# Row scales of the first linear attention moved from q and k to v, and a spread ratio in the gate pair, in a two-layer encoder kernel

## The chip, the cores and the metric

The kernel runs on one core of a Trainium2 chip. The metric is the device time of one execution in microseconds (us), taken as the median of several runs. The core has five engines with queues of their own, each working through its instructions in order: TensorE (PE, with its weight loads shown as PEld), VectorE (DVE), ScalarE (ACT), GpSimd (POOL) and SyncE (SP, which here only issues DMAs). They wait for each other through semaphores. What stands in each queue, and in which order, is fixed when the program is built.

## What is computed

Two layers of an encoder over 256 tokens of width 1024, in float32. What matters here is the first layer's beginning:

```python
u = rms_norm(h, g_mix_pre)
(gq, gk, gv, gg, ra_f, ra_b, aq, ak, av, gate_a, gate_b) = jnp.split(u @ w_in, offsets, axis=-1)
qh = gq * (GLA_DK ** -0.5); kh = gk; vh = gv           # 4 heads of 128, values of 256
# two directions of: scores = mask(q_dec @ k_intra^T); o = scores @ v + inter-chunk part
o_gla = rms_norm(o_f + o_b, g_gla_out)                 # per head
branch_a = (o_gla * silu(gg)) @ w_o_gla
branch_b = gqa_attention(q, k, v) @ w_o_attn           # 8 heads, 2 key/value heads, rope
mixed = sigmoid(gate_a) * branch_a + sigmoid(gate_b) * branch_b
h = h + rms_norm(mixed @ w_out, g_mix_post)            # then a SwiGLU FFN and an embedding step
```

## The kernel before, in words

**Tokens and halves.** The 256 tokens are two halves (`hf` 0 and 1) of 128, a token on each partition. `uT` holds the input of a layer transposed (features on partitions), split into a high part of type fp32r and the rest, so that a float32 product is three matmuls: high by high, high by low, low by high.

**Weights.** They stream through one class, `Stream`. A unit is 512 rows by 512 columns (1 MB): SP loads it into one of two `raw` buffers (L296), ACT casts it to fp32r (`wh`, L132) and DVE subtracts (`wl`, L132), both in two pieces of 128x1024. A `raw` buffer is free for the next load when DVE's second subtraction is done; `wh` and `wl` have four buffers each. Counted from 0, the layer's units 0 to 3 are the decay ranks and the attention's queries (`rq`), 4 and 5 the attention's keys and values (`kv`), 6 and 7 the linear attention's q, 8 and 9 its k (together `gqk`), 10 to 13 its v, 14 to 17 its output gate (`gg`), and then follow the units of gate A, the pair for gate B and `w_o_gla` in turn, in the order of the string `GATES` (21 is the last of gate A). On PE a `gqk` unit is 48 matmuls of 128x256, the others 24 of 128x512.

**The first layer's row scale.** In layer 0, `uT` is made from x before its RMS norm is known, and the factor r = 1/sqrt(mean(x^2)+eps) of each token (`rs[hf]`, made on POOL in `rstd`, L776 to L780, with `he` = 128 eps / r^2) is applied to what comes out of the products. Where tokens lie on partitions it is a scalar of the eviction. The linear attention's q and k come out with features on partitions and tokens along the row (`project_t`), so there the factor must be a row that is the same on every partition. `spread_rows` (L874) makes it: POOL writes a matrix of ones, DVE multiplies the identity by `rs[0]` and by `rs[1]` (L882), PE multiplies ones by these diagonals (two float32 products, four matmuls in the trace, L104 `aux_0kv`), ACT copies the result (L884). It is called right behind the `kv` products (L1090), so its matmuls stand in PE's queue between `kv` and `gqk`, and its two DVE instructions stand in DVE's queue behind what the scheduler put ahead of them. The four results of `gqk` are then evicted by DVE with a multiplication by that row (L1185); layer 1 evicts them on ACT (L1190, L1192).

**Around it.** Tasks (generators that yield a number of ticks) put the transposes, scores, softmax and output products of the attention (`attend`, `softmax`) and of the linear attention (`gla`: `decays`, `scores`, `outputs`) between the weight products. The keys are scaled by their norm on DVE (L1075), and the transposed decay ranks are copied to `raT` on DVE (L994). `outputs` (L1269) takes the sum of squares of each head, adds eps and raises to -1/2 on POOL (`inv_sqrt`).

**The gate pair.** Gate B is computed as a two-by-two block product with seven products (`seven`, L627) instead of eight. Its four blocks of the input are the two token halves by the two halves of the features; `whole` (L1380) adds high and low again, `sums` (L602) makes the four mixed forms and splits them, and two of the seven products (the sixth and the seventh) take their blocks straight from `uT`.

Of the kernel before, what the change touches and what calls it, by code (L numbers as in the profile page):

```python
# [27 lines left out]

WAIT_NEXT, WAIT_IN, WAIT_H = (7, 11), ((6, 9), (6, 6)), ((3, 5), (3, 5))
WAIT_MIX = 4, 6  # L30
W = dict(r=5, z=6, s0=4, s=3, s1=9, o0=1, o=1, k=4, q=3, a0=1, a1=4, a2=4, a3=1, g=6)

STEPS_FIRST = "00 10 01 11 02 12 03 13".split()
# [25 lines left out]
def trunk_kernel(ctx: ExitStack, tc: tile.TileContext, a: dict, out: bass.AP):  # L59
# [564 lines left out]

        return made, Task(make(), part[0])

    def seven(sp, forms, gated):  # L627

        made, task = forms
        quad = lambda hf, j: lambda k: sp.tok(4 * j + k, hf)  # L630
        form = lambda i: lambda k: [p[:, k, :] for p in made[i]]

        def add(out, x, y):
            nc.vector.tensor_tensor(out=out, in0=x, in1=y, op=ALU.add)

        (p1, v), (p3, p7) = (halves(mid()) for _ in range(2))
        c11, p5, o = acc(), acc(), []
        c12, c22 = p3, p7

        def product(i, then):  # L640

            o[:] = [acc()]
            times(o[0], form(i), True, then)

        def both():
            add(v, o[0], v)
            add(c12, v, p3)
            add(c22, v, p7)

        def last():  # L650
            vsub(v, p5, c22)
            gated(1, v, c22)

        times(c11, quad(0, 0), True, lambda: nc.scalar.copy(p1, c11))
        yield
        task.need()
        product(0, lambda: nc.scalar.copy(p3, o[0]))
        yield
        times(p5, form(1), True, lambda: vsub(v, p5, p1))
        yield  # L660
        product(2, lambda: nc.scalar.copy(p7, o[0]))
        yield
        product(3, both)
        yield
        times(c11, quad(0, 1), False, lambda: gated(0, c11, c12))
        yield
        times(p5, quad(1, 1), False, last)
        yield

    def project_t(sp):  # L670
# [87 lines left out]
    warm_up(WARM[1], True)  # L758
    uT = Split()
    ss = [small(2, "ss") for _ in range(2)]  # L760
    rs, he = ([small(1, tag, 2) for _ in range(2)] for tag in ("rs", "he"))
    ropes_first = []

    up_first = [mid()]
# [10 lines left out]
    def rstd(hf):  # L775
        on("pool", nc.gpsimd.tensor_scalar,  # L776
           out=rs[hf], in0=ss[hf][:, 0:1], scalar1=ss[hf][:, 1:2], scalar2=EPS, op0=ALU.add, op1=ALU.add)
        on("pool", nc.gpsimd.tensor_scalar, out=he[hf], in0=rs[hf], scalar1=P * EPS, scalar2=None, op0=ALU.mult)
        on("pool", nc.gpsimd.tensor_tensor, out=rs[hf], in0=rs[hf], in1=neghalf[:, 0:1], op=ALU.pow)
        last_pow[0] = line["pool"]  # L780

    def gains():
# [36 lines left out]
    def start():  # L819
        cut = lambda piece, c: [t[:, c] for t in piece]  # L820
        gains()
        for hf in range(2):
            turn(hf, 0)
        for hf in range(2):
            high(hf, 0)
        warm_up(WARM[2], True)
        turn(0, 1)
        turn(1, 1)
        turn(0, 2, 3)
        for c in RQ:  # L830
            on("act", nc.scalar.copy, *(t[:, slice(*c)] for t in unit_a[::2]))
        rest(0, 0)
        rest(1, 0)
        low(*cut(unit_a, slice(0, 288)))
        high(0, 1)
        high(1, 1)
        low(*cut(unit_a, slice(288, 1056)))
        on("act", nc.scalar.copy, unit_b[0], unit_b[2])
        rest(0, 1)
        rest(1, 1)  # L840
        high(0, 2, 3)
        low(*unit_b)
        rest(0, 2, 3)
        ws.load()
        unit_c, unit_d = ws.pieces()
        yield 2
        turn(1, 2, 3)
        high(1, 2, 3)
        rest(1, 2, 3)
        yield 4  # L850
        split_here(*unit_c)
        split_here(*unit_d)
        ws.load()
        for hf in range(2):
            square(hf, 0)
        yield 2
        turn(0, 4, 5, 6, 7)
        for hf in range(2):
            square_here(hf, 1)
            rstd(hf)  # L860
        ropes_first.extend(rope_tables(0))
        high(0, 4, 5, 6, 7)
        rest(0, 4, 5, 6, 7)
        yield 1
        turn(1, 4, 5, 6, 7)
        high(1, 4, 5, 6, 7)
        rest(1, 4, 5, 6, 7)
        for piece in ws.pieces():
            split_here(*piece)
        ws.load()  # L870
        ws.open = True
        ws.fill()

    def spread_rows():  # L874

        both = mid()
        diag, ones, out = both[:, 0:T], both[:, T : T + P], both[:, 512 : 512 + T]
        nc.gpsimd.memset(ones, 1.0)
        ps = aux()
        for hf in range(2):  # L880
            s = slice(hf * P, (hf + 1) * P)
            nc.vector.tensor_scalar(out=diag[:, s], in0=ident, scalar1=rs[hf], scalar2=None, op0=ALU.mult)  # L882
            mm(ps[:, s], ones, diag[:, s], True, True)
        nc.scalar.copy(out, ps[:, 0:T])  # L884
        return out

    def keep_embedding():

# [43 lines left out]
    for l in range(DEPTH):  # L932

        part[0] = f"{l}rq"
        rows, eps = ([None, None], [None, None]) if l else (rs, he)
        after_start = tc.issue_after(line["dma"].ins) if l == 0 else nullcontext()
        if l == 0:
            ropes = ropes_first
# [28 lines left out]
        def put_ranks(o, hf):  # L967
# [23 lines left out]
            ps = aux()  # L991
            for d in range(2):
                nc.tensor.transpose(ps[0:81, d * P : (d + 1) * P], r[:, d, 0:81], ident)
            nc.vector.tensor_copy(  # L994
                raT[:, :, hf * P : (hf + 1) * P], ps[0:81, 0 : 2 * P].rearrange("p (d t) -> p d t", d=2)
            )

# [6 lines left out]
        def put_q(hf, b, o):  # L1004
            qr, ss = qrs[hf], qss[hf]
            with tc.high_priority(EMPTY if l else EMPTY_FIRST):
                if b == 0:
                    ranks.append(Task(put_ranks(o, hf), part[0]))
                c0, c1 = RQ[b]
                lo = 32 if b == 0 else 0  # L1010
                n, hd = (c1 - c0 - lo) // P, max(c0 - 32, 0) // P
                src, dst = o[:, lo : c1 - c0], qr[:, hd * P : (hd + n) * P]

                with ws.behind(4 + hf, 0) if l == 0 else nullcontext():
                    head_ss(src, n, dst, ss[:, hd : hd + n])
                inv_sqrt(ss[:, hd : hd + n], n, 1.0, P * EPS, eps[hf])
                with ws.behind(4 + hf, 1) if l == 0 else nullcontext():
                    rope(src, n, ropes[0], hf, dst)

        def rq_step(o, hf, b, u):  # L1020
# [41 lines left out]
        def keys(o):  # L1062
            krs = []
            for hf in range(2):
                with tc.high_priority(EMPTY):
                    kr = t512()
                    ss = small(2, "kss")
                    head_ss(o[hf], 2, kr, ss)
                    inv_sqrt(ss, 2, 1.0 / P, EPS, eps[hf])
                    rope(o[hf], 2, ropes[1], hf, kr)  # L1070
                    s = slice(hf * 256, (hf + 1) * 256)
                    split_by(avh[:, s], avl[:, s], o[hf][:, 256:512], rows[hf])
                    for i in range(2):
                        s = slice(i * P, (i + 1) * P)
                        nc.vector.tensor_scalar(  # L1075
                            out=kr[:, s], in0=kr[:, s], scalar1=ss[:, i : i + 1], scalar2=None, op0=ALU.mult
                        )
# [9 lines left out]

        keys = Task(keys(project(uT)), f"{l}kv")
        if l == 0:
            spread = spread_rows()  # L1090


        aT = Split()
# [85 lines left out]
        for x in range(2):  # L1179
            o = project_t(uT)  # L1180
            for i in range(2):
                dst = qk[:, x, 2 * i : 2 * i + 2, :]
                src = o[i].rearrange("p (h t) -> p h t", t=T)
                if l == 0:
                    nc.vector.scalar_tensor_tensor(  # L1185
                        out=dst, in0=src, scalar=1.0 if x else P**-0.5,
                        in1=spread.unsqueeze(1).broadcast_to([P, 2, T]), op0=ALU.mult, op1=ALU.mult,
                    )
                elif x == 0:
                    nc.scalar.activation(dst, src, AF.Copy, bias=0.0, scale=P**-0.5)  # L1190
                else:
                    nc.scalar.copy(dst, src)  # L1192
# [76 lines left out]
        def outputs(hf, pr):  # L1269
# [3 lines left out]
            for i in range(2):  # L1273
# [7 lines left out]
                nc.scalar.activation(  # L1281
                    on[:, hf, c], oh, AF.Square, scale=1.0 / 16.0, accum_out=ss[:, i : i + 1]
                )
            inv_sqrt(ss[:, 0:2], 2, 1.0, EPS)
            for i in range(2):
                hd = 2 * pr + i
                scale_gain(
# [32 lines left out]
        )  # L1320
        for j in range(2):
            for hf, o in enumerate(project(uT)):
                split_by(*(t[:, hf, j * 512 : (j + 1) * 512] for t in v), o, rows[hf])
        valued[0] = True


# [32 lines left out]
        def sigmoid(br, hf, j, src):  # L1359
            if sgate[br] is None:  # L1360
                sgate[br] = big().rearrange("p (s c) -> p s c", s=2)
            with tc.issue_after(last_exp[0].ins):
                by = {} if rows[hf] is None else {"scale": rows[hf]}
                nc.scalar.activation(sgate[br][:, hf, j * 512 : (j + 1) * 512], src, AF.Sigmoid, **by)

        def blocks(sp, then):

            for j in range(2):
                o = [acc(), acc()]
                for kh in range(2):  # L1370
# [6 lines left out]
                    ws.done()  # L1377
                    yield

        def whole():  # L1380

            res = [halves(mid()) for _ in range(2)]
            for hf in range(2):
                for j in range(2):
                    hi, lo = (t.bitcast(F32) for t in uT.at(4 * j, 4, hf * P, P))
                    nc.vector.tensor_tensor(
                        out=res[hf][j].rearrange("p (k t) -> p k t", t=P), in0=hi, in1=lo, op=ALU.add
                    )
            return res

        def gate_b(hf, c0, c1):
# [3 lines left out]
        def merge(br):  # L1395
# [15 lines left out]
        steps = {  # L1411
            "u": blocks(uT, lambda j, hf, o: sigmoid(0, hf, j, o)),
            "m": blocks(gT, merge(0)),
            "s": seven(uT, forms, gate_b),
        }
        for x in GATES:
            if x == "m":
# [236 lines left out]
```

## Time and profile before

| | |
|---|---|
| time, median of 3 runs | 934.36 us (932.77 to 934.6) |
| the profiled execution | 932.52 us, of which its span is 930.7 us |
| busy share of the span | PE 98%, PEld 84%, DVE 85%, ACT 62%, POOL 9% |
| mean granted TensorE clock | 0.992 |
| bytes moved | 173.44 MB, 186 GB/s over the span |

Every engine name in a row is followed by the line of the kernel. `wl_0kv` is a tile named `wl` made in the part `0kv`: the digit is the layer, the rest the stage whose code asked for it, which for weights is often the stage before the one that uses them. `out<-in` names what is written and read. A row of the timeline has the start, the time from the start to the end of a group of equal instructions, the engine, the line, the operation, the tiles, the shapes and the count, and in brackets how long the engine had been idle and what ended that.

### The profile page before, as it was taken

To read this page: it belongs to the slowest core of one execution; us is meant where nothing else is said; L and a number is where in the kernel's file an instruction comes from. 1 tells how busy PE (TensorE), PEld (TensorE's weight loads), DVE (VectorE), ACT (ScalarE), POOL (GpSimd) and SP (SyncE) were. 2 spreads that over 40 slices of the span, in tenths; PEclk is the share of its full clock that TensorE was granted. 3 is DMA by queue.
4 is the path that set the end of the run, shared out by engine and by line. 5 is a ranking of instruction groups with operands and counts; after the bars stand their busy time and mean duration, and the time that the engine had idled before them with its cause. 6 is when DMAs were issued, how large, how long until landed. Compare 5 with 4: busy or idle time off the path is not lost.

```text
span 930.7 us, 12440 instructions
## 1 busy us (share of the span) xinstructions
PE 911.6 (98%) x4676; PEld 777.3 (84%) x4676; DVE 787.6 (85%) x1012; ACT 578.8 (62%) x959; POOL 83.8 (9%) x145
## 2 busy tenths in 40 slices
PE   9879999999999999999999999999999999999996
PEld 8779888888888888888899988888888888888886
DVE  7868989996678998999788789899876799989984
ACT  6647777664476656575676586765644766656563
POOL 2700101130010000000013101110000100000000
PEclk9989999999999999999999999999999999999999
DMA  8552356547468474727666533555573855556361
GB/s 291 182 198 91 97 177 227 165 148 261 136 212 286 136 271 158 271 77 242 246 215 203 179 132 107 165 181 180 182 227 110 280 193 189 217 176 238 126 237 45
DMA packets 88679, 173.44 MB, mean 186 GB/s; under 512 B 3422, under 2 KB 26470, under 8 KB 88108
## 3 DMA queue, kind: packets, MB, share of 16 engines
q1 hardware_dynamic: 88460, 172.40, 55.0%
q8 instruction: 36, 0.59, 0.3%
q10 hardware_dynamic: 160, 0.27, 0.1%
q14 instruction: 23, 0.19, 0.1%
HBM read 169.50 MB, written 3.15 MB: 186 GB/s over the span
## 4 chain that ended last, share of the span: by engine, by line
PE 87%; DVE 4%; DMA 3%; ACT 2%; issue 2%; POOL 1%; SPq 0%; POOLq 0%; DVEq 0%; ACTq 0%
PE acc_0ffnin L120 12%; PE acc_1ffnin L120 11%; PE acc_1gate L120 7%; PE acc_0gate L120 7%; PE acc_0ffnin L104 6%; PE acc_1ffnin L104 6%; PE acc_0gqk L120 3%; PE acc_0wout L120 2%; PE acc_1gqk L120 2%; PE acc_1ple L120 2%; PE acc_1gg L120 2%; PE acc_0gg L120 2%; PE acc_0v L120 2%; PE acc_0merge L120 2%; PE acc_1merge L120 2%; PE acc_1rq L120 2%
## 5 line engine op out<-in xcount | busy, mean ns | idle before, releaser
L104 PE MATMUL acc_0ffnin<-wh_0ffnin,big_0ffnin 128*128 128x512 f32 x176 | 56.9, 393 | 0.0
L104 PE MATMUL acc_1ffnin<-wh_1ffnin,big_1ffnin 128*128 128x512 f32 x176 | 56.8, 392 | 0.0
L132 ACT CAST wh_1ffnin<-raw_1ffnin 128x1024 fp32r<-128x1024 f32 x38 | 38.5, 1049 | 26.0 <-PE acc_1ffnin L104 10.4
L132 ACT CAST wh_0ffnin<-raw_0ffnin 128x1024 fp32r<-128x1024 f32 x38 | 38.4, 1049 | 23.9 <-PE acc_0ffnin L104 9.3
L132 DVE TENSOR_TENSOR wl_1ffnin<-raw_1ffnin,wh_1ffnin 128x1024 fp32r<-128x1024 f32 x38 | 45.0, 1220 | 8.3 <-ACT wh_1ffnin L132 8.2
L132 DVE TENSOR_TENSOR wl_0ffnin<-raw_0ffnin,wh_0ffnin 128x1024 fp32r<-128x1024 f32 x38 | 44.7, 1219 | 7.3 <-ACT wh_0ffnin L132 7.2
L120 PE MATMUL acc_1ffnin<-wh_1ffnin,big_1wout 128*128 128x512 f32 x168 | 42.5, 393 | 0.0
L120 PE MATMUL acc_0ffnin<-wh_0ffnin,big_0wout 128*128 128x512 f32 x168 | 42.5, 393 | 0.0
L104 PEld LDWEIGHTS acc_0ffnin<-wh_0ffnin,big_0ffnin 128*128 128x128 f32 x176 | 33.0, 188 | 7.1 <-DVE big_0ffnin L132 0.5
L104 PEld LDWEIGHTS acc_1ffnin<-wh_1ffnin,big_1ffnin 128*128 128x128 f32 x176 | 33.0, 188 | 6.7
L132 DVE TENSOR_TENSOR wl_0ffnin<-lent_0ffnin,wh_0ffnin 128x1024 fp32r<-128x1024 f32 x30 | 35.8, 1216 | 1.8 <-ACT wh_0ffnin L132 1.8
L132 DVE TENSOR_TENSOR wl_1ffnin<-lent_1ffnin,wh_1ffnin 128x1024 fp32r<-128x1024 f32 x30 | 35.8, 1217 | 1.8 <-ACT wh_1ffnin L132 1.6
L120 PEld LDWEIGHTS acc_0ffnin<-wh_0ffnin,big_0wout 128*128 128x128 f32 x168 | 31.1, 188 | 6.2
L120 PEld LDWEIGHTS acc_1ffnin<-wh_1ffnin,big_1wout 128*128 128x128 f32 x168 | 31.1, 188 | 6.2
L132 ACT CAST wh_1ffnin<-lent_1ffnin 128x1024 fp32r<-128x1024 f32 x30 | 30.7, 1053 | 7.3 <-PE acc_1ffnin L104 3.9
L132 ACT CAST wh_0ffnin<-lent_0ffnin 128x1024 fp32r<-128x1024 f32 x30 | 30.7, 1054 | 7.1 <-PE acc_0ffnin L104 3.9
L104 PE MATMUL acc_0ffnin<-wl_0ffnin,big_0ffnin 128*128 128x512 f32 x88 | 34.2, 389 | 0.0
L104 PE MATMUL acc_1ffnin<-wl_1ffnin,big_1ffnin 128*128 128x512 f32 x88 | 34.2, 389 | 0.0
L132 DVE TENSOR_TENSOR wl_1gate<-raw_1gate,wh_1gate 128x1024 fp32r<-128x1024 f32 x20 | 23.5, 1218 | 6.7 <-ACT wh_1gate L132 6.7
L132 ACT CAST wh_1gate<-raw_1gate 128x1024 fp32r<-128x1024 f32 x20 | 20.0, 1047 | 12.9 <-DMA raw_1gate<-in_w_o_attn_dram 6.1
L132 DVE TENSOR_TENSOR wl_0gate<-raw_0gate,wh_0gate 128x1024 fp32r<-128x1024 f32 x20 | 23.6, 1223 | 4.9 <-ACT wh_0gate L132 4.8
L132 ACT CAST wh_0gate<-raw_0gate 128x1024 fp32r<-128x1024 f32 x20 | 20.0, 1050 | 11.3 <-DMA raw_0gate<-in_w_o_attn_dram 5.4
(702 smaller groups left out, 2693.4 us busy)
## 6 DMA issues: line engine op xcount, KB each, us to landing
raw_0ffnin<-in_w_ffn_out_dram SPq DMA_DIRECT2D x11, 1024.0 KB, 5.4
raw_1ffnin<-in_w_ffn_out_dram SPq DMA_DIRECT2D x11, 1024.0 KB, 5.3
lent_0ffnin<-in_w_ffn_in_dram SPq DMA_DIRECT2D x6, 1024.0 KB, 7.7
lent_1ffnin<-in_w_ffn_in_dram SPq DMA_DIRECT2D x6, 1024.0 KB, 6.5
raw_0v<-in_w_in_dram SPq DMA_DIRECT2D x4, 1024.0 KB, 5.3
raw_0gate<-in_w_o_gla_dram SPq DMA_DIRECT2D x4, 1024.0 KB, 5.1
raw_0gate<-in_w_o_attn_dram SPq DMA_DIRECT2D x4, 1024.0 KB, 5.2
raw_0wout<-in_w_ffn_in_dram SPq DMA_DIRECT2D x8, 512.0 KB, 5.3
```

The source lines that it names most:

```text
L104: return nc.tensor.matmul(o, lhsT, rhs, start=start, stop=stop)
L120: nc.tensor.matmul(o, x, y, start=start and n == 0, stop=stop and n == len(seq) - 1, **kw)
L132: return nc.scalar.copy(hi, src), nc.vector.tensor_tensor(out=lo, in0=src, in1=hi.bitcast(F32), op=ALU.subtract)
```

## The change

For layer 0 only:

- **q and k of the linear attention are no longer scaled by r.** They are evicted on ACT as in layer 1. The factor of k goes to v, whose eviction takes r^2 (`rows2`); the factor of q is dropped, because the outputs are normalised per token and head, with eps replaced by eps/r^2 (`em`).
- **`spread_rows` goes.** `scales` makes `em`, `r2` = r^2 and `rho` = r(half 1)/r(half 0) times a constant on POOL, five instructions of 128x1 behind `rstd`. A task `spread` transposes `rho`, broadcast over 128 columns, with one PE instruction 12 ticks later, and ACT copies it, with the constant taken out, to `even` (a row of 128 ratios, the same on every partition) in the buffer of layer 0's first rope table.
- **In the gate pair** the second token half is multiplied by `even` (two DVE products of 128x512 in `whole`), so that both halves take `rows[0]` in the sigmoid. The seventh product then needs that scaled block too: `alone`, one more buffer of type `mid` and one more split (ACT cast and DVE subtraction of 128x512).
- **From DVE to ACT**: the four evictions, the scaling of the keys by their norm (four of 128x128) and the two copies to `raT`.
- **Order**: the third block of the attention's queries of half 1 has its rope held behind the split of unit 6 instead of unit 5 (`ws.behind`).

```diff
-    def seven(sp, forms, gated):
+    def seven(sp, forms, gated, alone=()):
...
-        times(p5, quad(1, 1), False, last)
+        times(p5, (lambda k: [x[:, k * P : (k + 1) * P] for x in alone]) if alone else quad(1, 1), False, last)
...
+    def scales():
+        for hf in range(2):
+            on("pool", nc.gpsimd.tensor_scalar, out=em[hf], in0=he[hf], scalar1=1.0 / P, scalar2=None, op0=ALU.mult)
+            on("pool", nc.gpsimd.tensor_tensor, out=r2[hf], in0=rs[hf], in1=rs[hf], op=ALU.mult)
+        on("pool", nc.gpsimd.tensor_scalar,
+           out=rho, in0=he[0], scalar1=rs[0], scalar2=rs[1], op0=ALU.mult, op1=ALU.mult)
         last_pow[0] = line["pool"]
...
-    def spread_rows():
-        both = mid()
-        diag, ones, out = both[:, 0:T], both[:, T : T + P], both[:, 512 : 512 + T]
-        nc.gpsimd.memset(ones, 1.0)
+    def spread():
+        yield WAIT_SPREAD
         ps = aux()
-        for hf in range(2):
-            s = slice(hf * P, (hf + 1) * P)
-            nc.vector.tensor_scalar(out=diag[:, s], in0=ident, scalar1=rs[hf], scalar2=None, op0=ALU.mult)
-            mm(ps[:, s], ones, diag[:, s], True, True)
-        nc.scalar.copy(out, ps[:, 0:T])
-        return out
+        nc.tensor.transpose(ps[:, 0:P], rho.broadcast_to([P, P]), ident)
+        nc.scalar.activation(even, ps[:, 0:P], AF.Copy, bias=0.0, scale=1.0 / (P * EPS))
...
-            nc.vector.tensor_copy(
+            (nc.vector.tensor_copy if l else nc.scalar.copy)(
                 raT[:, :, hf * P : (hf + 1) * P], ps[0:81, 0 : 2 * P].rearrange("p (d t) -> p d t", d=2)
...
-                with ws.behind(4 + hf, 1) if l == 0 else nullcontext():
+                with ws.behind(4 + hf + (hf == 1 and b == 2), 1) if l == 0 else nullcontext():
                     rope(src, n, ropes[0], hf, dst)
...
+                        if l == 0:
+                            nc.scalar.activation(kr[:, s], kr[:, s], AF.Copy, bias=0.0, scale=ss[:, i : i + 1])
+                            continue
...
         if l == 0:
-            spread = spread_rows()
+            even = small(512, "rope0", 1)[:, 0:P]
+            Task(spread(), f"{l}kv")
...
-                if l == 0:
-                    nc.vector.scalar_tensor_tensor(
-                        out=dst, in0=src, scalar=1.0 if x else P**-0.5,
-                        in1=spread.unsqueeze(1).broadcast_to([P, 2, T]), op0=ALU.mult, op1=ALU.mult,
-                    )
-                elif x == 0:
+                if x == 0:
                     nc.scalar.activation(dst, src, AF.Copy, bias=0.0, scale=P**-0.5)
...
-            inv_sqrt(ss[:, 0:2], 2, 1.0, EPS)
+            inv_sqrt(ss[:, 0:2], 2, 1.0, EPS, eps_out[hf])
...
-                split_by(*(t[:, hf, j * 512 : (j + 1) * 512] for t in v), o, rows[hf])
+                split_by(*(t[:, hf, j * 512 : (j + 1) * 512] for t in v), o, rows2[hf])
...
-                by = {} if rows[hf] is None else {"scale": rows[hf]}
+                by = {} if l else {"scale": rows[0 if br else hf]}
...
+            if l == 0:
+                for j in range(2):
+                    t = res[1][j].rearrange("p (k t) -> p k t", t=P)
+                    vmul(t, t, even.unsqueeze(1).broadcast_to([P, 4, P]))
+                alone.extend(halves(mid(F32R)))
+                split(*alone, res[1][1])
```

More of the change, by code (lines that the diff above doesn't have):

```diff
@@ L30 @@
 WAIT_MIX = 4, 6
+WAIT_SPREAD = 12
 W = dict(r=5, z=6, s0=4, s=3, s1=9, o0=1, o=1, k=4, q=3, a0=1, a1=4, a2=4, a3=1, g=6)
@@ L760, in trunk_kernel @@
     ss = [small(2, "ss") for _ in range(2)]
-    rs, he = ([small(1, tag, 2) for _ in range(2)] for tag in ("rs", "he"))
+    rs, he, em, r2 = ([small(1, tag, 2) for _ in range(2)] for tag in ("rs", "he", "em", "r2"))
+    rho = small(1, "rho", 1)
     ropes_first = []
@@ L779, in rstd @@
         on("pool", nc.gpsimd.tensor_tensor, out=rs[hf], in0=rs[hf], in1=neghalf[:, 0:1], op=ALU.pow)
+        last_pow[0] = line["pool"]
+    def scales():
[4 more added lines that the diff above has]
+           out=rho, in0=he[0], scalar1=rs[0], scalar2=rs[1], op0=ALU.mult, op1=ALU.mult)
         last_pow[0] = line["pool"]
@@ L860, in start @@
             rstd(hf)
+        scales()
         ropes_first.extend(rope_tables(0))
@@ L934, in trunk_kernel @@
         part[0] = f"{l}rq"
-        rows, eps = ([None, None], [None, None]) if l else (rs, he)
+        rows, eps, eps_out, rows2 = ([[None, None]] * 4) if l else (rs, he, em, r2)
         after_start = tc.issue_after(line["dma"].ins) if l == 0 else nullcontext()
@@ L1378, in blocks @@
                     yield
+        alone = []
         def whole():
@@ L1413, in trunk_kernel @@
             "m": blocks(gT, merge(0)),
-            "s": seven(uT, forms, gate_b),
+            "s": seven(uT, forms, gate_b, alone),
         }
```

## The prediction

> **What bounds the kernel now.** I read the share of each engine in slices of the span first, from the profile's page.
>
> ```profile
> PE   9879999999999999999999999999999999999996
> PEclk9989999999999999999999999999999999999999
> ```
>
> TensorE is at nine tenths or more in nearly all of the 40 slices of 23.3 us. The second and third slices, 23 to 70 us, are among the few that aren't, and in the third its clock dips too. So a change pays only if it shortens PE's queue or takes away time in which PE stands still. The second view is PE's waits from 45 us to 930 us (engine, line, what it waited for, total us, times, longest).
>
> ```profile
> PE aux_0kv L104 <- DVE mid_0kv L882: 9.7, 1, 9.7
> PE aux_1at L104 <- DVE mid_1at L132: 0.2, 1, 0.2
> ```
>
> These are all of them: behind the start, PE waits once for 9.7 us, for the diagonals of `spread_rows`, and never again for more than 0.2. The third view is the timeline around that wait.
>
> ```profile
> 41.77 1.07 PE L120 MATMUL acc_0kv<-wl_0rq,big_start 128*128 128x512 f32 x4
> 41.89 1.21 DVE L132 TENSOR_TENSOR wl_0rq<-raw_start,wh_0rq 128x1024 fp32r<-128x1024 f32 x1
> 43.69 0.41 DVE L994 CAST raT<-aux_0rq 81x256 fp32r<-81x256 f32 x1
> 46.49 0.86 DVE L1075 TENSOR_SCALAR t_0kv<-t_0kv,kss_0kv 128x128 f32<-128x128 f32 x4
> 47.27 2.35 DVE L132 TENSOR_TENSOR wl_0rq<-raw_0rq,wh_0rq 128x1024 fp32r<-128x1024 f32 x2
> 49.88 2.35 DVE L132 TENSOR_TENSOR wl_0kv<-raw_0rq,wh_0kv 128x1024 fp32r<-128x1024 f32 x2
> 52.15 0.47 DVE L882 TENSOR_SCALAR mid_0kv<-ident,rs_start 128x128 f32<-128x128 f32 x2
> 52.57 1.20 PE L104 MATMUL aux_0kv<-mid_0kv 128*128 128x128 f32 x4 [9.73 <-DVE mid_0kv L882]
> 55.92 2.36 DVE L132 TENSOR_TENSOR wl_0kv<-raw_0rq,wh_0kv 128x1024 fp32r<-128x1024 f32 x2 [3.30 <-ACT wh_0kv L132]
> ```
>
> PE ends `kv` at 41.77 + 1.07 = 42.84. The next in its queue are the four matmuls on the diagonals. DVE makes those at 52.15, because by its order they stand behind the splits of units 7 and 8. Yet unit 6, which PE could multiply at 42.84, is split at 41.89 + 1.21 = 43.10. The wait comes from an order, not from missing data. The fourth view is of windows (length, then busy us and count of PE, PEld, DVE, ACT, POOL, then PEclk, DMA share, GB/s).
>
> ```profile
> 45.00:50.00 5.00, 0.00 (x0) 0.00 (x0) 5.00 (x13) 1.98 (x3) 0.47 (x1) 0.54 0.52 192
> 55.00:60.00 5.00, 5.00 (x42) 5.00 (x41) 2.36 (x2) 2.40 (x3) 0.00 (x0) 0.93 0.49 150
> 42.84:82.81 39.97, 30.24 (x242) 30.23 (x243) 29.97 (x58) 20.24 (x42) 1.78 (x3) 0.87 0.49 160
> 82.81:152.27 69.46, 69.46 (x384) 59.60 (x383) 63.22 (x109) 53.85 (x112) 10.35 (x16) 1.00 0.39 123
> 513.26:541.33 28.07, 28.07 (x238) 27.97 (x236) 21.37 (x45) 18.11 (x40) 1.11 (x3) 1.00 0.50 165
> 541.33:611.27 69.94, 69.76 (x385) 59.74 (x384) 61.99 (x108) 53.74 (x113) 10.07 (x16) 1.00 0.38 121
> ```
>
> Rows 3 and 5 are the same stage in the two layers, from the end of `kv` to the first `aux_gla` matmuls. 238 matmuls took 28.07 us in layer 1; 242 (four more: the spread) took 39.97 in layer 0, 11.90 longer. The waits and the timeline give 9.73 of it as idle and 1.20 as the spread; the other 0.97 is the clock, which the first two rows show at 0.54 and not yet full (0.93) after 55. Rows 4 and 6, up to the gate stage, differ by 0.5 us.
>
> **The change part by part.** *The wait goes (−9.73), the spread matmuls go (−1.20), the clock stays up (−0.97).* Instead of four matmuls PE gets one transpose of `rho`, twelve ticks later; the four spread matmuls at half clock took 0.30 each, so at full clock +0.15; its operand is there long before (below). That makes −11.75 if PE can go on at 42.84. What is late next? Unit 6's low part: PE does eight high matmuls first, and needs it at about 43.8; it was there at 43.10. A `gqk` unit is 48 matmuls of 28.07/238 = 0.118, so 5.7 us. By the new order (which a listing of the built program gives) unit 7's low part is needed at about 50.0; by the rows above it was there at 47.27 + 2.35 = 49.62 even with all of DVE's old work ahead of it, of which 0.41 (L994) and 0.86 (L1075) now go. Unit 8's is needed at 57.1 and was there at 49.88 + 2.35 = 52.23. Unit 9's is needed at about 64.5 and was there at 58.28. So the weights follow, by the old times already.
>
> *DVE and ACT.* The prices of what moves, from groups of the trace (out<-in, shapes, count | busy, mean ns | idle before):
>
> ```profile
> L1185 DVE SCALAR_TENSOR_TENSOR big_0gqk<-acc_0gqk,mid_0kv 128x512 f32<-128x512 f32 x4 | 2.7, 685 | 0.6 <-PE acc_0gqk L120 0.6
> L994 DVE CAST raT<-aux_0rq 81x256 fp32r<-81x256 f32 x2 | 0.8, 408 | 0.0
> L1386 DVE TENSOR_TENSOR mid_0gate<-big_start 128x512 f32<-128x512 f32 x4 | 2.6, 681 | 0.0
> L132 DVE TENSOR_TENSOR mid_0gate<-mid_0gate,mid_0gate 128x512 fp32r<-128x512 f32 x3 | 1.9, 679 | 0.0
> ```
>
> ```profile
> L1190 ACT ACTIVATE big_1gqk<-acc_1gqk 128x512 f32<-128x512 f32 x2 | 1.2, 600 | 1.3 <-PE acc_1gqk L120 1.3
> L132 ACT CAST mid_1at<-aux_1at 128x512 fp32r<-128x512 f32 x12 | 6.6, 583 | 2.6 <-PE aux_1at L1133 1.7 <-PE aux_1at L1146 0.9
> L965 ACT ACTIVATE t_1kv<-acc_1kv 128x128 f32<-128x128 f32 x4 | 1.1, 270 | 1.6 <-POOL kss_1kv L462 1.6
> L132 ACT CAST big_1kv<-aux_1kv 128x256 fp32r<-128x256 f32 x2 | 0.8, 380 | 0.0
> ```
>
> DVE loses 2.7 + 0.8 + 0.9 (L1075) + 0.5 (L882) = 4.9 us. It gains, at 0.68 each, two products with `even` and the low part of `alone`: 2.0 us. A product with a repeated row could cost more than the plain one; L1185, which reads such a row, took 685 ns, so it doesn't. ACT gains four evictions (2.4), two `raT` copies (81x256; between 0.27 for 128x128 and 0.58 for 128x512, taken as the 128x256 cast, 0.38), four scalings (1.1), the copy to `even` (0.3) and the cast of `alone` (0.6), and loses L884 (128x256, 0.4): 4.8 us. ACT was busy for 20.24 of 39.97 us in row 3, so on average there is room even in 28; the three rows of casts below show it idle for 1.0 to 2.9 us ahead of loads, and the `raT` copies fall into such gaps. If that cover were gone the two copies would hold PE by 0.8 at most.
>
> [...]
>
> *Tight places.* I laid the new order out by hand with the old durations. (a) The transposes of the scaled keys: PE arrives at 50.6; on ACT the four scalings now stand behind the first cast of unit 8, which waits for its load. (b) The first scores: PE arrives at 42.84 + 14.76 = 57.6, and DVE has the low part of the transposed keys at 57.2 to 57.6. (c) The first output products of the attention, at which layer 1 waited for the 0.2 us of the row above. For (a), and for ACT's gaps, these are the rows:
>
> ```profile
> 35.34 1.06 ACT L132 CAST wh_0rq<-raw_start 128x1024 fp32r<-128x1024 f32 x1 [1.97 <-DMA raw_start<-in_w_in_dram]
> 41.81 2.00 ACT L132 CAST wh_0rq<-raw_0rq 128x1024 fp32r<-128x1024 f32 x2 [1.03 <-DMA raw_0rq<-in_w_in_dram]
> 48.49 1.99 ACT L132 CAST wh_0kv<-raw_0rq 128x1024 fp32r<-128x1024 f32 x2 [2.87 <-DMA raw_0rq<-in_w_in_dram]
> ```
>
> If the load lands no earlier than it did, the cast ends at 48.49 + 1.0, and an eviction of 128x256 (0.38) and two scalings (0.54) behind it at 50.4: just in time. I take 0.5 us of new waits for (a) to (c) together, between 0 (all arrive as laid out) and 2 (each misses by one split of 128x512, 0.68).
>
> *POOL and SP.* Five more instructions of 128x1 stand on POOL between `rstd` and the rope tables.
>
> ```profile
> 17.01 0.23 POOL L141 TENSOR_SCALAR he_start<-rs_start 128x1 f32<-128x1 f32 x1
> 17.32 0.57 POOL L141 TENSOR_TENSOR rs_start<-rs_start,neghalf 128x1 f32<-128x1 f32 x1
> 21.61 0.74 POOL L716 TENSOR_TENSOR rope_start<-mid_start 128x256 f32<-128x256 f32 x1 [3.72 <-DMA mid_start<-in_g_q_norm_dram]
> ```
>
> At 0.23 to 0.57 each they take 1.2 to 2.9 us, inside the 3.72 us for which POOL then waits for a DMA. Without that cover they would delay the ropes by as much. The change adds no DMA; SP's order of issues is the same.
>
> *The gate stage.* The new work of `whole` sits ahead of weight splits in DVE's queue there.
>
> ```profile
> 168.38 1.21 DVE L132 TENSOR_TENSOR wl_0gate<-raw_0gate,wh_0gate 128x1024 fp32r<-128x1024 f32 x1
> 173.38 1.07 PE L120 MATMUL acc_0gate<-wl_0gate,big_start 128*128 128x512 f32 x4
> ```
>
> This split ends at 169.59 and PE uses it at 173.38: 3.8 us of slack. DVE is 2.0 later, ACT's cast of `alone` and the sigmoid moved behind it take about 1 more, and 0.7 is left. I take no cost; if it misses, it costs some tenths.
>
> **Sum:** −9.73 − 1.20 − 0.97 + 0.15 + 0.5 = −11.25 against the profiled execution's 932.52: 921.3 (span 919.5). The median of the runs is 934.36, 1.84 above it; the same shift gives **923.1**.
>
> **Rivals.** *DVE becomes the bound (gain 4.6).* With PE's wait, DVE loses the time in which it got ahead. From 42.84 to 152.27 it was busy for 29.97 + 63.22 = 93.2 of 109.4 us. After the change that is 90.3 of 98.2: only 7.9 idle. Layer 1, without any wait of that size, had 83.4 busy of 98.0: 14.6 idle. If layer 0 needs the same idle time, since DVE waits for ACT's casts and PE's results and can't use it, the stretch is 14.6 − 7.9 = 6.7 longer: −4.6, 929.8. For it: row 4 shows DVE at 91%. Against it: in the same row PE never waited, at DVE's 91%, and the hand layout keeps every split from unit 7 to 13 ahead of its use. I give 17%.
>
> [...]
>
> *The change doesn't do what it says: the wait only moves (within 0.2%).* PE runs ahead to the next thing that comes at a fixed time, a load or a rope that stands where it stood. Then it stops at 50 or 57 for what it saved. Against it: the old times of units 7 to 9, above, are all early enough. I give 3%; the time is 934.4.
>
> *ACT's queue holds PE (slower).* ACT takes 4.8 us more in front of its casts, and its queue is in order: an eviction or a scaling that waits for PE holds the casts behind it, and a cast that waits for a load holds the evictions. Without PE's wait there is no pause in which ACT catches up. The price is a cast pair, 2.0 us (48.49 row), for each unit that PE then waits for; six units from unit 8 to 13 make 12 us, over the 11.75 saved: 935 to 936. It decides from 1.9 us for each unit. For it: (a) above, and ACT at 53.85 of 69.46 in row 4. Against it: layer 1's ACT does the same four evictions and PE waits for 0.2 there. I give 5%.
>
> **How the numbers follow.** The forecast, −11.75 to −9.5 with the new waits between 0 and about 2, has 75% (922.6 to 924.9 as a median). That the medians differ from the profiled runs by the 1.84 in one case and not in the other widens it down to 921. With DVE as the bound, 929.8, the cases hold 92%, so the range is 921.0 to 930.0. About 0.2%, 1.9 us, is what a measurement of this kernel can tell from no change: faster 0.92, same 0.03, slower 0.05.
>
> **What would show it.** In the profile after: no wait at 42.84 and `gqk` from there, the first `aux_gla` matmuls at 71.0 to 71.6, PEclk 1.0 from 40 to 60, PE's waits together below 1 us, a span near 919.5. The sum is wrong if PE's waits name `wl` or `mid` tiles between 50 and 152 for several us (DVE), or casts and `raT`, `t_0kv` written by ACT (ACT's queue). It is wrong at the gate if PE waits at about 162 us in the new time for DVE's split.

## The result and the profile after

The changed kernel takes 921.18 us (median of 4 runs, 920.84 to 921.63), the one before 934.48 (4 runs, 932.77 to 934.78): a ratio of 0.9862, 95% interval 0.9845 to 0.9879. By the medians that is 13.3 us less. By the two profiled executions it is 11.2: the span is 919.5 where it was 930.7. Why the two differ is taken up under "Why the prediction was right".

The page of the changed kernel, PE's share and clock in the 40 slices:

```profile
PE   9999999999999999999999999999999999999996
PEclk9999999999999999999999999999999999999999
```

The dips between 23 and 70 us are gone, in the busy share and in the clock. PE's waits from 40 to 920 us (engine, line, what it waited for, total us, times, longest) are now these:

```profile
PE aux_1at L105 <- DVE mid_1at L133: 0.2, 1, 0.2
PE aux_0gla L105 <- ACT big_0gla L1286: 0.2, 1, 0.2
```

The 9.7 us on `aux_0kv` have left the list and one wait of 0.2 is new. The timeline shows what follows `kv` (start, length):

```profile
41.73 1.07 PE L121 MATMUL acc_0kv<-wl_0rq,big_start 128*128 128x512 f32 x4
42.64 1.12 PE L121 MATMUL acc_0gqk<-big_start,wh_0rq 128*128 128x256 f32 x8
...
49.39 1.27 ACT L1082 ACTIVATE t_0kv<-t_0kv,kss_0kv 128x128 f32<-128x128 f32 x4
...
50.38 0.27 PE L1093 MATMUL aux_0kv<-ident,t_0kv 128*128 128x128 f32 x1
...
56.71 0.42 DVE L133 TENSOR_TENSOR big_0kv<-aux_0kv,big_0kv 128x256 fp32r<-128x256 f32 x1
...
57.36 1.36 PE L105 MATMUL aux_0at<-big_0kv,mid_0at 128*128 128x256 f32 x10
```

PE goes from `kv` into `gqk` without a pause. The next rows are the prediction's tight places (a) and (b): the scalings on ACT begin at 49.39 and the first transpose of a scaled key runs at 50.38; the low part of the keys ends at 57.13 and the scores that need it run at 57.36. The forecast, laid out by hand, had both to within 0.3 us. Windows of the changed kernel, columns as before:

```profile
45.00:50.00 5.00, 5.00 (x44) 5.00 (x43) 3.81 (x10) 2.97 (x8) 2.45 (x3) 1.00 0.62 201
55.00:60.00 5.00, 5.00 (x44) 5.00 (x44) 3.93 (x8) 2.72 (x4) 0.00 (x0) 1.00 0.86 290
42.80:70.95 28.15, 28.15 (x239) 28.15 (x239) 24.69 (x46) 22.95 (x52) 3.65 (x4) 1.00 0.67 217
70.95:140.99 70.04, 69.88 (x384) 59.58 (x383) 62.51 (x108) 53.64 (x111) 12.16 (x14) 1.00 0.39 124
```

The stage from `kv` to the first `aux_gla` takes 28.15 us for 239 matmuls, where layer 1 took 28.07 for 238: what layer 1 showed is what layer 0 got. The next stage takes 70.04, 0.58 more than before.

POOL was not as forecast (the changed kernel, start and length):

```profile
17.86 2.07 POOL L142 TENSOR_SCALAR em_start<-he_start 128x1 f32<-128x1 f32 x1
19.90 1.26 POOL L142 TENSOR_TENSOR r_start<-rs_start 128x1 f32<-128x1 f32 x1
...
21.48 1.41 POOL L142 TENSOR_SCALAR rho_start<-he_start,rs_start,rs_start 128x1 f32<-128x1 f32 x1
22.84 1.76 POOL L717 TENSOR_TENSOR rope_start<-mid_start 128x256 f32<-128x256 f32 x1
24.56 1.16 POOL L721 TENSOR_TENSOR rope_start<-mid_start 128x64 f32<-128x64 f32 x4
...
26.38 1.16 POOL L721 TENSOR_TENSOR rope_start<-mid_start 128x64 f32<-128x64 f32 x4
```

The five instructions lasted from 17.86 to about 22.9, 5.0 us instead of 1.2 to 2.9, so the 3.72 us of waiting did not cover them: the rope tables start at 22.84, not 21.61. Little of these 1.23 us is left at the tables' end, 26.38 + 1.16 = 27.54 against 27.33 before, because the first four instructions of L721 took 1.16 here and 3.19 before (L720 there). PE ends `kv` at 42.80 (42.84 before), so the late start did not delay it. In a second profile of the changed kernel (`after_again` below) `rho` took 0.33 instead of 1.41 and the tables start at 22.09.

The gate stage:

```profile
159.19 2.35 DVE L133 TENSOR_TENSOR wl_0gate<-raw_0gate,wh_0gate 128x1024 fp32r<-128x1024 f32 x2
162.10 1.07 PE L121 MATMUL acc_0gate<-wl_0gate,big_start 128*128 128x512 f32 x4
```

The split is ready at 161.54 and used at 162.10: 0.56 us of slack (0.7 was laid out), no wait.

### The profile page after: what moved, and what is told of

The parts are those of the page before. It is cut to its first block, busy times and chain, and to the rows that moved or that the text cites. A ratio compares the mean times of both kernels' runs of the same rounds, so it can differ in the third digit from the quotient of the medians.

```text
span 919.5 us, 12425 instructions
## 1 busy us (share of the span) xinstructions
PE 909.8 (99%) x4673; PEld 775.9 (84%) x4673; DVE 783.3 (85%) x1003; ACT 582.7 (63%) x970; POOL 91.7 (10%) x149
## 4 chain that ended last, share of the span: by engine, by line
PE 91%; DVE 3%; ACT 2%; DMA 2%; issue 1%; POOL 1%; ACTq 0%; POOLq 0%; DVEq 0%; SPq 0%
PE acc_0ffnin L121 12%; PE acc_1ffnin L121 11%; PE acc_0gate L121 7%; PE acc_1gate L121 7%; PE acc_0ffnin L105 7%; PE acc_1ffnin L105 7%; PE acc_0gqk L121 2%; PE acc_0wout L121 2%; PE acc_1gqk L121 2%; PE acc_1ple L121 2%; PE acc_1gg L121 2%; PE acc_0v L121 2%; PE acc_0merge L121 2%; PE acc_1merge L121 2%; PE acc_0gg L121 2%; PE acc_0rq L121 2%
```

## The experiments

Two questions were open: was it only the wait in PE's queue that the change took away, or was relief of DVE needed as well; and which part of the change did it. Times of one group below come from the same chip, beside their own runs of the kernel before.

**Only the diagonals made early** (edit to the kernel before; `diagonals()` is called behind `rstd`, and `spread_rows` keeps its four matmuls where they were):

```diff
+    def diagonals():
+        on("pool", nc.gpsimd.memset, ones, 1.0)
+        for hf in range(2):
+            on("pool", nc.gpsimd.tensor_scalar, out=diag[:, hf * P : (hf + 1) * P], in0=ident,
+               scalar1=rs[hf], scalar2=None, op0=ALU.mult)
...
-            nc.vector.tensor_scalar(out=diag[:, s], in0=ident, scalar1=rs[hf], scalar2=None, op0=ALU.mult)
```

> The kernel before with one edit: the diagonals and the ones of spread_rows are made on POOL, right behind rstd, so that the four spread matmuls find them ready where they stand; DVE keeps the four evictions, the key scalings and the raT copies. Theory A (PE's queue: only the place of what PE waited for costs): the wait of 9.73 us goes, the clock's 0.97 too, and the spread at full clock costs 0.6 instead of 1.20, so 11.3 us less than before by the profiles; all but 0.45 us of the whole change. Rival D (DVE becomes the bound unless its 4.4 us of work are taken from it as well): PE waits for wl tiles or for mid tiles by DVE between 45 and 90 us, 4 to 7 us in all, so only 5 to 7 us less than before.

Measured: 921.2 us, ratio 0.9856 (0.984 to 0.9872), span 918.8. PE's waits from 40 us on, all of them:

```profile
PE aux_1at L104 <- DVE mid_1at L132: 0.2, 1, 0.2
```

Theory A. The four matmuls stay, the evictions, scalings and copies stay on DVE, and the time is that of the whole change. On POOL the two diagonals took 3.65 us (0.47 on DVE), in the time in which POOL otherwise waited for a DMA; the rope tables start at 21.90.

**DVE's work given back** (edit to the changed kernel: `raT` by `nc.vector.tensor_copy`, the keys scaled by `nc.vector.tensor_scalar`, the four evictions by `nc.vector.tensor_scalar`, in layer 0 too).

> The changed kernel with the work that went from DVE to ACT given back to DVE (four evictions 128x512, four key scalings 128x128, two raT copies; 4.4 us). Theory A: DVE has the room, PE's new waits stay below 1 us in all, the time within 0.5 us of the changed kernel. Rival D: 3 to 5 us slower than the changed kernel, with PE waiting for DVE between 45 and 152 us.

Measured: 921.08 us, ratio 0.9859 (0.9843 to 0.9875). No new wait over 0.4 us. The stretch from `kv` to the gate stage:

```profile
42.84:141.01 98.17, 98.00 (x621) 87.70 (x620) 90.76 (x164) 73.75 (x155) 14.32 (x18) 1.00 0.47 151
```

DVE is idle for 98.17 − 90.76 = 7.4 us, about the 7.9 at which the prediction's first rival expected 6.7 us of loss, and nothing is lost. The relief of DVE isn't needed once the spread is out of the way.

**The same with the rope's place undone too** (`ws.behind(4 + hf, 1)` again).

> The changed kernel with DVE's work given back and the rope's place undone too: of the change only the spread is gone and the gate pair changed; DVE's queue up to unit 8 stands as before. Theory A (as forecast: the old times of the splits are early enough): unit 7's low part comes at 49.6 and is needed at 50.0, so within 0.6 us of the changed kernel. Rival D: PE waits for unit 7's split by 1 to 3 us.

Measured: 921.43 us, ratio 0.9869 (0.9854 to 0.9884). This is the prediction's claim that the old times of the splits are early enough, taken by itself; it holds: unit 7's split ends at 49.86 (49.62 before) and PE first uses it at 50.81.

**The old spread put back into the changed kernel** (`spread_rows()` as before, called behind the keys' products, its result unused).

> The changed kernel with the old spread_rows put back behind the keys' products, its result unused. Theory A: PE waits again for the second diagonal, which stands behind splits in DVE's queue; with 1.3 us less ahead of them 8 to 10 us of wait, 1.2 of matmuls and 1.0 of clock: 10 to 12 us slower than the changed kernel. Rival D: the wait matters less than DVE's load, under 5 us slower.

Measured: 923.44 us, ratio 0.9882 (0.9867 to 0.9898): 2.3 us above the changed kernel (1.9 by the spans), not 10 to 12. That looks like rival D, and isn't. The timeline:

```profile
43.05 0.27 DVE L894 TENSOR_SCALAR mid_0kv<-ident,rs_start 128x128 f32<-128x128 f32 x1
43.47 0.46 PE L105 MATMUL aux_0kv<-mid_0kv 128*128 128x128 f32 x2
...
51.64 0.28 DVE L894 TENSOR_SCALAR mid_0kv<-ident,rs_start 128x128 f32<-128x128 f32 x1
...
51.98 0.49 PE L105 MATMUL aux_0kv<-mid_0kv 128*128 128x128 f32 x2
```

The scheduler, with less on DVE, put the first diagonal ahead of unit 7's split, and held the second pair of matmuls back in PE's queue to 51.98. PE waits for neither. What the 1.9 us consist of was not taken apart; all of it is there at the first `aux_gla` (72.82 against 70.95). So the experiment did not put the wait back. It points to the place that the scheduler gives to two DVE instructions of 0.27 us, and that asked for the next two.

**The small edits alone, spread and evictions kept** (edit to the kernel before: `raT` and key scalings to ACT, and the rope behind unit 6).

> The kernel before, spread_rows and all its evictions kept, with only the small edits of the change: raT copies and key scalings on ACT, and the one rope held behind unit 6's split. In the built program the first diagonal now stands on DVE ahead of unit 7's split, and the second behind unit 8's, with its matmuls further back in PE's queue. Theory A2 (what costs is where the scheduler puts the two diagonals and the matmuls on them, and several edits move them): the wait goes, the spread runs at full clock, 10 to 12 us less than before. Rival R2 (the spread has to leave: the evictions that need it hold PE): PE waits at 53 or later, under 5 us less than before.

Measured: 922.35 us, ratio 0.9877 (0.9862 to 0.9892). Its only wait at that place:

```profile
PE aux_0kv L104 <- DVE mid_0kv L882: 0.6, 1, 0.6
```

Theory A2: 11.3 us of the gain without touching the row scale. What moved is this:

```profile
42.96 0.27 DVE L882 TENSOR_SCALAR mid_0kv<-ident,rs_start 128x128 f32<-128x128 f32 x1
43.38 0.46 PE L104 MATMUL aux_0kv<-mid_0kv 128*128 128x128 f32 x2 [0.58 <-DVE mid_0kv L882]
...
51.26 0.28 DVE L882 TENSOR_SCALAR mid_0kv<-ident,rs_start 128x128 f32<-128x128 f32 x1
51.76 0.39 PE L104 MATMUL aux_0kv<-mid_0kv 128*128 128x128 f32 x2
```

The first diagonal now stands ahead of the split of unit 7. The second does not, but its two matmuls stand further back in PE's queue, so that PE works on `gqk` in between.

**Only the two moves to ACT, the rope left** (the same without the edit of `ws.behind`).

> The kernel before with raT copies and key scalings on ACT alone, the rope where it was. In the built program both diagonals stand behind unit 7's split, ahead of unit 8's. Theory A2: PE still waits, but for one unit's split less and 1.3 us less of small work: from 42.8 to about 48.8, 6 us instead of 9.7, and the clock still falls, so 3 to 4 us less than before. Rival R2: less than 1.5 us less, only the 1.3 us of work that left DVE.

Measured: 928.89 us, ratio 0.9947 (0.9932 to 0.9962), span 926.9, 3.8 less than before's 930.7. The diagonals and the windows:

```profile
48.17 0.48 DVE L882 TENSOR_SCALAR mid_0kv<-ident,rs_start 128x128 f32<-128x128 f32 x2
48.60 1.20 PE L104 MATMUL aux_0kv<-mid_0kv 128*128 128x128 f32 x4 [5.96 <-DVE mid_0kv L882]
```

```profile
45.00:50.00 5.00, 1.40 (x6) 1.43 (x7) 4.27 (x11) 3.39 (x8) 0.83 (x2) 0.65 0.64 206
50.00:55.00 5.00, 5.00 (x32) 5.00 (x31) 2.23 (x3) 2.14 (x4) 0.00 (x0) 0.67 0.91 306
```

One split less stands ahead of the diagonals, the wait is 5.96 (6 expected), and the clock falls all the same (0.65 over 45 to 50 us, 0.67 over the next 5). With 9.73, 5.96, 0.58 and 0 us of wait (before, this run, the one above it and the early diagonals) the first `aux_gla` comes at 82.81, 79.54, 72.38 and 71.49. Take off the wait and what the slow clock behind it costs (estimated at 1.6 and 2.3 us in the first two: half of the time to its return, in which the granted clock was 0.50, see the last section): 71.5, 71.2, 71.8 and 71.5. The time follows the wait and the clock behind it. From the start of the gate stage to the end the profiles of all these kernels take 777.9 to 779.3 us, so part of a difference between two spans can come from there.

**The hole filled** (edit to the kernel before: 38 idle matmuls ahead of the spread's).

> The kernel before with 38 matmuls of 128x512 (bf16, result unused, 0.23 us each, 8.6 us) ahead of the spread's in PE's queue: PE's hole is filled with work that waits for nothing. If the lower clock behind the hole comes from the idle time: PEclk stays at 1.0, the spread takes 0.6 instead of 1.20 and gqk 0.97 less, so 1.6 us less than before. If the clock has another cause: the same as before within 0.3 us.

Measured: 931.29 us, ratio 0.9973 (0.9963 to 0.9983), span 929.1, 1.6 less. Window and timeline:

```profile
45.00:50.00 5.00, 5.00 (x25) 2.25 (x23) 5.00 (x13) 1.97 (x4) 0.78 (x2) 1.00 0.53 199
```

```profile
52.95 0.68 PE L104 MATMUL aux_0kv<-mid_0kv 128*128 128x128 f32 x4 [1.86 <-DVE mid_0kv L885]
```

With PE busy the clock stays at 1.00 (over the same 5 us it was 0.54 before), through the 1.86 us of wait that are left too, and the spread takes 0.68 instead of 1.20: here the idle time causes the slow clock. By the chain, 1.0 of the 1.6 us is there at the first `aux_gla` (81.80, was 82.81), less than forecast, since the spread starts 0.38 us later than before (52.95 against 52.57). The other 0.6 lies behind the start of the gate stage, within the differences given above; that the span gives just the 1.6 expected is luck.

**The gate pair left alone** (edit to the changed kernel: no products with `even`, no `alone`, `rows[hf]` in the sigmoid), and then **without `rho` and its transpose too**:

> The changed kernel without its edit of the gate pair: no products with the ratio row, no alone, each half takes its own factor in the sigmoid as before. Theory A: the edit's 2.0 us of DVE and 0.6 of ACT lie in slack; within 0.3 us of the changed kernel. Rival G: they hold a split or an eviction that PE waits for; 0.5 to 1.5 us faster than the changed kernel.

> The changed kernel without its edit of the gate pair, as in the run before, and without rho and its transpose, which nothing needs then. Theory A: the transpose (0.11 us of PE) and one POOL instruction go; 0.1 us less than the run without the gate edit, 0.6 us less than the changed kernel, 920.6. Rival: the scheduler orders the queues of the start otherwise; off by up to 1 us either way.

Measured: 920.68 us (920.56 to 920.81), ratio 0.9858 (0.9842 to 0.9875), and 920.69, ratio 0.9859 (0.9844 to 0.9875). Beside the second, on the same chip, the changed kernel itself:

> The changed kernel itself, beside the lean version on the same chip. Expected 921.2 with a spread of about 1 us, and 0.5 to 0.6 us above the lean version, which has no gate edit.

Measured: 921.52 us (921.25 to 921.8), ratio 0.9869 (0.9855 to 0.9883). The stage that is 70.04 long in the changed kernel reads in the one without the gate edit:

```profile
71.14:140.60 69.46, 69.46 (x383) 59.63 (x383) 62.63 (x109) 55.01 (x113) 11.95 (x16) 1.00 0.40 127
```

and the changed kernel's timeline has PE's new wait in it:

```profile
134.14 0.62 ACT L133 CAST mid_0gate<-mid_0gate 128x512 fp32r<-128x512 f32 x1 [0.94 <-DVE mid_0gate L126]
...
134.66 0.38 ACT L1286 ACTIVATE big_0gla<-aux_0gla 128x256 f32<-128x256 f32 x1
...
135.18 0.97 PE L105 MATMUL aux_0gla<-v_0v,big_0gla 128*128 128x256 f32 x6 [0.16 <-ACT big_0gla L1286]
```

Rival G, small: the edit costs 0.58 us in this stage. The five profiles of kernels with the edit have 70.00 to 70.04 there, the eight of kernels without it 69.45 to 69.47. The cast of a gate half on ACT, there because DVE's products with `even` came first, holds an eviction; 0.16 of it is a wait, the rest lies in a changed order of PE's queue, which no run took apart. The transpose is worth nothing that can be measured. The version without the gate edit beats both kernels; it is 0.5 to 0.8 us under the changed one.

**The kernel before once more**, for a second profile:

> The kernel before itself, for a second profile. Its median is 933.6 to 934.5 while its profiled execution took 932.5. If the difference sits in the one long wait (the second split or its load comes later in most executions), the wait reads 10 to 12 us in a profile of a slower execution, and the stages behind it are the same. If it sits elsewhere, the wait reads 9.7 again and some other stage is 1 to 2 us longer. If the profile is a 932.5 again, this stays open.

Measured: 933.91 us (ratio 1.0002, 0.9993 to 1.0011), and this time the profiled span is 933.5:

```profile
PE aux_0kv L104 <- DVE mid_0kv L882: 10.5, 1, 10.5
```

```profile
42.65 1.99 ACT L132 CAST wh_0rq<-raw_0rq 128x1024 fp32r<-128x1024 f32 x2 [1.83 <-DMA raw_0rq<-in_w_in_dram]
...
53.40 1.20 PE L104 MATMUL aux_0kv<-mid_0kv 128*128 128x128 f32 x4 [10.52 <-DVE mid_0kv L882]
```

```profile
55.00:60.00 5.00, 5.00 (x29) 5.00 (x28) 2.36 (x2) 2.00 (x3) 0.00 (x0) 0.60 0.54 205
```

The load of unit 7 landed 0.84 us later (42.65 against 41.81), the diagonals with it, and the clock took longer to come back: 0.60 over 55 to 60, where the first profile had 0.93. By the chain the first `aux_gla` starts at 84.72 instead of 82.81, 1.9 us later. The other 0.9 us of the longer span lie behind the gate stage's start.

## Why the prediction was right

- **The wait goes, and nothing takes its place.** PE starts `gqk` at once, and the first `aux_gla` matmuls come at 70.95, 11.86 earlier than before; forecast were 11.75 without new waits. The span, 919.5, is the forecast's to the tenth, and that is partly luck: of the 0.5 us of new waits only 0.16 came, and the gate edit, for which the forecast took no cost, filled their place with 0.58.
- **The clock stays up.** Shown by the filled hole: 1.00 throughout, with PE kept busy.
- **DVE has the room.** Shown twice: with all its work back, and with its old order too, the time is the same. In the changed kernel DVE was busy for 24.69 + 62.51 = 87.2 of 98.2 us from 42.80 to 140.99, not for the 90.3 of the forecast; but with 90.8 in the run with its work back it did not hold PE either. The rival took layer 1's 14.6 us of idle time for an amount that DVE needs, and 7.4 were enough.
- **ACT's queue** held PE once, for 0.16 us, at the place where the cast of the gate pair went in. Place (c) of the forecast did not show.
- **POOL was mis-sized**: 5.0 us in one profile of the changed kernel and 4.0 in the other, instead of 1.2 to 2.9, beyond its cover by 1.23 and 0.48. It cost PE 0.2 us at most: the rope tables ended 0.2 and 0.5 us later than in the first profile of before, and PE ended `kv` at 42.80 and 43.06, where the two profiles of before have 42.84 and 42.88.
- **The term that failed is the last one, "the same shift".** The 1.84 us between the profiled execution of before and its median was carried over to the changed kernel. It was no constant: the kernel before scatters from 932.6 to 937.0 over the runs of all groups, and the quoted profile, 932.52, was quicker than any of them. Two profiles show part of the reason: the long wait hangs on when a load lands (41.81 and 42.65 us, with 9.73 and 10.52 of wait), and what it costs on how long the clock takes to recover (3.1 and 5.6 us from PE's start). The runs agree: the 15 of 49 with a mean granted clock of 0.991 or less have spans of 932.8 on average, the others 931.6. The rest of the scatter is not explained. The changed kernel has no such wait, its runs lie within 1 us (920.84 to 921.8), and its profile agrees with its median; but the kernel with the old spread put back has no such wait either and reached 925.5 once, so the wait is not the only source. So 923.1 was 1.9 too high, and the gain by medians is 13.3. The forecast had named this case and widened its range down to 921.0 for it; 921.18 lies just inside.
- **What the prediction took for the cause was one step short.** It said that the wait comes from an order, and was right; but it gave the credit to the removal of the spread. The small edits alone give 11.3 us, and diagonals made on an idle engine all of it. Each does the same: no matmul at the head of PE's queue is left to wait behind DVE's splits for an instruction of 0.27 us.

## What to carry to other kernels

When the bound engine has one long hole, ask what the late operand stands behind before rewriting the mathematics: here two instructions, made early on an idle engine, were worth as much as a new scaling scheme, though they took 3.65 us there instead of 0.47. Compare a stage with its twin in another layer: 28.07 us for layer 1's 238 matmuls forecast the 28.15 that layer 0 then took, down from 39.97. And don't carry the distance between one profile and a median over to a kernel in which the source of the scatter is gone; an "undo" experiment under a scheduler must be read in the trace first, since it may not put back what it was meant to.

## What the hardware showed

The time to the clock's return varied between two executions of the same kernel: 10.24 and 13.65 us from its fall in the two profiles of before. These are windows of half a microsecond in which the granted clock changed, two each from the first profile of before, the second one and the run with only the two moves (PEclk is the third number from the end; it was 1.00 ahead of the first window and behind the second, and 0.50 between them):

```profile
45.00:45.50 0.50, 0.00 (x0) 0.00 (x0) 0.50 (x3) 0.35 (x1) 0.47 (x1) 0.95 1.04 315
55.50:56.00 0.50, 0.50 (x5) 0.50 (x5) 0.08 (x1) 0.50 (x2) 0.00 (x0) 0.81 1.05 406
45.00:45.50 0.50, 0.00 (x0) 0.00 (x0) 0.30 (x1) 0.50 (x3) 0.23 (x1) 0.81 0.94 328
58.50:59.00 0.50, 0.50 (x4) 0.50 (x4) 0.50 (x1) 0.00 (x0) 0.00 (x0) 0.54 0.00 0
46.00:46.50 0.50, 0.00 (x0) 0.00 (x0) 0.50 (x3) 0.50 (x3) 0.00 (x0) 0.97 1.04 401
53.00:53.50 0.50, 0.50 (x5) 0.50 (x5) 0.00 (x0) 0.07 (x1) 0.00 (x0) 0.71 0.38 57
```

A mean of 0.95 over 45.00 to 45.50 puts the fall at 45.45. In this way the clock was low from 45.45 to 55.69, from 45.31 to 58.96 and from 46.47 to 53.29, that is for 10.24, 13.65 and 6.82 us. These are 3, 4 and 2 times 3.41: in these three executions the return of the clock lies a whole number of steps of 3.41 us behind its fall. PE started again at 52.57, 53.40 and 48.60 and had the full clock 3.1, 5.6 and 4.7 us later. Counted from the fall, 3.1 us of the running step were left at the first of these starts, and the clock rose at its end; with 2.1 and 1.3 left, at the other two, it rose only at the end of the next. By this count 0.83 us of later start, in the second profile of before, missed a step, and the clock stayed low for 2.4 us longer behind it. Three cases are few, and what decides at the end of a step whether the clock rises was not tried.

POOL instructions of one element on each partition took 0.20 to 2.07 us in one and the same row of five. The first two were long in both profiles of the changed kernel (2.07 and 1.26, 2.08 and 1.26), the fifth in one (1.41 and 0.33). What made them long was not tried.
